# SSM operands put in order by block copies on chip, SSM products in column halves, and the cached keys' gain moved to the sampled queries

## The chip, the cores and the metric

The kernel runs on one core of a Trainium2 chip. A core has a matrix engine (TensorE, PE in the profile; its weight loads are listed as PEld), three engines for elementwise work (VectorE or DVE, ScalarE or ACT, GpSimd or POOL) and a queue engine that issues DMAs (SyncE, SP). ACT issues DMAs too. Each engine takes its own instructions in order and waits for the others by semaphores. The metric is the device time of one execution in microseconds; the median of several runs is compared.

## What is computed

One step of one decoder layer for 256 prompt tokens and 8 x 4 sampled tokens, d_model 2048, all in float32:

```python
x = x + 0.5 * swiglu(rms_norm(x))                 # first feed-forward, d_ff 5632
u, q, k, v = split(rms_norm(x) @ w_in)            # 1024 | 1024 | 256 | 256
y_ssm  = s5_mixer(u)     # 64 groups: 16 channels, 64 complex states; scan over positions
y_attn = window_attention(rms_norm(q, q_norm), rms_norm(k, k_norm), v)   # 16 heads, window 128
x = x + concat(rms_norm(y_ssm), rms_norm(y_attn)) @ w_out
x = x + 0.5 * swiglu(rms_norm(x))                 # second feed-forward
# s5_mixer:
h[t] = lam_bar * h[t-1] + B_bar u[t]
y = gelu(Re(C h) + D u);  y = y * sigmoid(y @ w_glu)
```

The sampled tokens see 128 cached keys of their sequence (already normed) and the 4 new ones. The kernel leaves the gain `q_norm` and the factor 1/8 out of the queries and applies both, as the column `qg`, to the other side of the score product.

## The kernel before

All 288 tokens (the sampled first in each group) stand as the columns of 128-row tiles. Every big product is an f32 product made of three passes over fp32r halves: for each weight piece of 128x1024, ScalarE casts the high half `wh` (L122), VectorE subtracts to get the low half `wl` (L123), and TensorE makes 24 products of 128x288 (L288 to L290).

**Slots.** The class `Weights` sets the order of the work. `W.next()` (one slot) issues the cast and subtraction of the piece two slots ahead (`split_ahead`), the loads of pieces five ahead, and then every function that was put in this slot with `W.at(slot, f)` in the order in which they were put; then the caller issues the slot's 24 products. `W.spread(slot, gen)` runs a generator one step a slot; with `last=True` its first step goes to the end of its slot. So side work stands in the queues of all engines between the big products, and what it waits for holds up what stands behind it on the same engine.

**The mixer** (`mix`, slots counted from `base`) projects in this order, two slots each: key pair 0, eight tiles of u, key pair 1, two tiles of v, eight tiles of q. Then 32 slots of `w_out`. R, the norm of x, is ready some slots in; until then evictions are held back (`Hold`).

**The SSM, tile j of 8.** The eviction (L756, VectorE) leaves u with channels on the partitions, for 4 quarters of 32 channels, and columns by position in a chunk of four. The products need it with 32 partitions for each position and the quarters side by side. Before, this order is made through DRAM: `ssm_u_store` (L759, issued on ACT's queue) and four loads of 32 partitions (L765, on SP's queue). In `ssm_state` (L790) eight matmuls of 128x128 by 128x72 give the chunk inputs; VectorE rotates them (L796 to L804), scans (L807, L808), rotates back (L817 to L821), with two products on POOL (L815, L816) and small copies on ACT and POOL. `ssm_out` (L830 to L832) makes twelve such matmuls, and ACT takes the gelu (L834). The result goes back to channel order through DRAM again: four stores (L840, ACT's queue), one load (L844, SP's queue) and, behind it on SP, the load of the gate weights `gl` (L846). `ssm_glu` multiplies by `gl` (L851), and `y_split` (L735 to L745) casts, squares and adds up. `state_done` and `ssm_done` free memory for the attention. With s = base + 2j + 5 the steps stand at s (store of u, first table load), s+2 (load of u, decay, rotation table), s+4 (state, four steps), s+6, s+9 (out), s+10, s+11 (store and load of y) and s+13 (gate).

**Attention, step i of 8** (a pair of heads). `q_square` (ACT), `scores`: sums of squares of the queries as two matmuls with the squares as the weights and two columns of `bones` (L1003), an inverse root in 12 small POOL instructions (`row_rsqrt`, L956 to L959), products with the keys (L1013), scaling (L1019), distance bias (L1023), softmax (L969 to L984, its last multiplication on POOL), then `probs_t` (transposes, L1032) and `pv` (L1045). The keys `kG` have been multiplied by `qg` on POOL (L909). For each key pair p, `sample` does the same for the sampled tokens with cached keys `ck`, which `cache_gain` multiplies by `qg` on POOL (L1060), and cached values (L1116).

## Time and profile before

| | |
|---|---|
| median of 3 runs | 1881.68 us (1880.63 to 1883.83) |
| the profiled execution | 1881.9 us, span 1880.1 us |
| PE busy | 1863.0 us (99%) |
| DVE, ACT, POOL busy | 1211.9, 850.6, 300.8 us |
| the 14400 big products (L288 to L290) | busy 4127.5 us by the sum of rows, each overlapping the next |
| SSM products, L790 and L830 to L832 | 320 instructions |
| granted TensorE clock | 1.00 |

The profile is one execution. A row of its groups names the line, the engine, the operation, what it writes and reads, its shape and its count, then busy time and mean length. The shape of a TensorE instruction has in front the part of the 128x128 array that it uses: `128*64` is all 128 rows and 64 columns. Lengths on TensorE are those of pipelined instructions: the next one starts before the last ends, so costs are read from starts. The matmuls of f32 stand in the trace as two instructions each. In the timeline, a row has its start, its length, and in brackets the idle time before it with what ended it.

### The profile page before, as it was taken

How to read it: one execution, taken by the hardware profiler on the slowest of the kernel's cores; microseconds unless marked ns; L12 is line 12 of the kernel's file. 1: busy time of each engine (PE TensorE's matmuls, PEld its weight loads, DVE VectorE, ACT ScalarE, POOL GpSimd, SP SyncE). 2: the span in 40 equal slices, each digit the busy share in tenths (PEclk: the TensorE clock that was granted, in tenths of full speed). 3: DMA queues.
4: the chain of work that ended last, by engine and by line, in shares of the span. 5: the costliest groups of instructions: out<-in, count | busy, mean ns of one | idle time of the engine just before them, and what ended most of it. 6: DMA issues, size and time to landing. Idle time of an engine off the chain costs nothing.

```text
span 1880.1 us, 37660 instructions
## 1 busy us (share of the span) xinstructions
PE 1863.0 (99%) x15264; PEld 1848.9 (98%) x15264; DVE 1211.9 (64%) x1877; ACT 850.6 (45%) x1337; POOL 300.8 (16%) x450
## 2 busy tenths in 40 slices
PE   9999999999999999999999999999999999999999
PEld 8999999999999999999988999999999999999999
DVE  6677667666667755687888885555555555555555
ACT  6443444444444444643476554433444334434433
POOL 3201011000100100211468650000000000000000
PEclk9999999999999999999999999999999999999999
DMA  7555656656665665778744456556655565556555
GB/s 265 198 181 165 217 179 213 196 170 218 213 200 171 213 213 156 238 246 290 239 137 133 158 176 183 180 165 183 191 180 171 170 197 180 167 167 205 180 162 170
DMA packets 123054, 359.04 MB, mean 191 GB/s; under 512 B 22496, under 2 KB 30688, under 8 KB 121696
## 3 DMA queue, kind: packets, MB, share of 16 engines
q1 hardware_dynamic: 114672, 340.48, 57.7%
q10 hardware_dynamic: 8208, 16.16, 2.5%
q8 instruction: 119, 1.95, 0.4%
q14 instruction: 55, 0.45, 0.1%
HBM read 338.40 MB, written 20.22 MB: 191 GB/s over the span
## 4 chain that ended last, share of the span: by engine, by line
PE 93%; DVE 2%; DMA 2%; POOL 2%; ACT 1%; issue 1%; SPq 0%; ACTq 0%; POOLq 0%; DVEq 0%
PE main L290 30%; PE main L288 30%; PE main L289 30%; DVE wl L123 1%; PE main L790 0%; DMA U<-ud 0%; PE main L832 0%; PE main L831 0%; PE main L621 0%; PE main L627 0%; PE main L830 0%; ACT wh L122 0%; POOL x L1153 0%; DMA out_kT<-s 0%; DVE sm_m L969 0%
## 5 line engine op out<-in xcount | busy, mean ns | idle before, releaser
L123 DVE TENSOR_TENSOR wl<-raw,wh 128x1024 fp32r<-128x1024 f32 (+2 forms) x677 | 751.7, 1111 | 453.9 <-ACT wh L122 451.6
L288 PE MATMUL main<-xh,wh 128*128 128x288 f32 x3136 | 902.5, 288 | 1.7 <-ACT xh L214 1.2
L290 PE MATMUL main<-xh,wl 128*128 128x288 f32 x3136 | 897.8, 286 | 0.7 <-DVE wl L123 0.6
L289 PE MATMUL main<-xl,wh 128*128 128x288 f32 x3136 | 897.3, 286 | 0.9 <-DVE xl L215 0.9
L122 ACT CAST wh<-raw 128x1024 fp32r<-128x1024 f32 (+2 forms) x677 | 636.9, 942 | 505.2 <-PE main L289 352.6
L288 PEld LDWEIGHTS main<-xh,wh 128*128 128x128 f32 x3136 | 592.8, 189 | 3.5 <-ACT xh L214 1.7
L289 PEld LDWEIGHTS main<-xl,wh 128*128 128x128 f32 x3136 | 592.8, 189 | 1.9 <-DVE xl L215 1.5
L290 PEld LDWEIGHTS main<-xh,wl 128*128 128x128 f32 x3136 | 592.7, 189 | 1.7 <-DVE wl L123 0.8
L288 PE MATMUL main<-hh,wh 128*128 128x288 f32 x1664 | 477.9, 287 | 1.2 <-DVE t L1152 0.7
L289 PE MATMUL main<-hl,wh 128*128 128x288 f32 x1664 | 476.0, 286 | 0.6 <-DVE hl L741 0.6
L290 PE MATMUL main<-hh,wl 128*128 128x288 f32 x1664 | 476.0, 286 | 0.0
L288 PEld LDWEIGHTS main<-hh,wh 128*128 128x128 f32 x1664 | 314.5, 189 | 1.8 <-DVE t L1152 0.9
L289 PEld LDWEIGHTS main<-hl,wh 128*128 128x128 f32 x1664 | 314.5, 189 | 1.0 <-DVE hl L741 0.8
L290 PEld LDWEIGHTS main<-hh,wl 128*128 128x128 f32 x1664 | 314.5, 189 | 0.2 <-DVE wl L123 0.2
L362 POOL TENSOR_TENSOR s<-s,R 128x288 f32<-128x288 f32 x88 | 70.7, 803 | 1139.2 <-ACT s L361 1139.2
L371 ACT CAST hh<-h 128x288 fp32r<-128x288 f32 x88 | 38.0, 432 | 222.9 <-DVE h L370 222.9
L361 ACT ACTIVATE s<-t 128x288 f32<-128x288 f32 x88 | 39.0, 443 | 219.9 <-DVE t L360 219.9
L392 DVE SCALAR_TENSOR_TENSOR x<-main,x 128x288 f32<-128x288 f32 x128 | 58.4, 456 | 39.9 <-PE main L290 39.5
L370 DVE TENSOR_TENSOR h<-main,s 128x288 f32<-128x288 f32 x88 | 40.1, 456 | 55.9 <-PE main L290 55.6
L360 DVE TENSOR_TENSOR t<-main,R 128x288 f32<-128x288 f32 x88 | 40.1, 456 | 45.1 <-PE main L290 44.7
L372 DVE TENSOR_TENSOR hl<-h,hh 128x288 fp32r<-128x288 f32 x88 | 40.3, 458 | 43.8 <-ACT hh L371 43.8
L224 POOL TENSOR_TENSOR acc<-acc,sq 128x288 f32<-128x288 f32 x45 | 45.3, 1006 | 46.0 <-ACT sq L220 45.1
(268 smaller groups left out, 913.9 us busy)
## 6 DMA issues: line engine op xcount, KB each, us to landing
raw<-in_w_gu SPq DMA_DIRECT2D x349, 512.0 KB, 3.9
raw<-in_w_dn SPq DMA_DIRECT2D x128, 384.0 KB, 3.1
raw<-in_w_dn SPq DMA_DIRECT2D x128, 320.0 KB, 3.2
raw<-in_w_in SPq DMA_DIRECT2D x40, 512.0 KB, 4.5
raw<-in_w_out SPq DMA_DIRECT2D x32, 512.0 KB, 3.4
mats<-stage ACTq DMA_DIRECT2D x8, 1536.0 KB, 6.8
mb<-mats SPq DMA_DIRECT2D x8, 768.0 KB, 6.2
ma<-mats SPq DMA_DIRECT2D x8, 512.0 KB, 4.2
```

Of the source, the lines that this page charges most:

```text
L122: self.nc.scalar.copy(wh[:, :n], t[:, :n])
L123: self.nc.vector.tensor_tensor(wl[:, :n], t[:, :n], wh[:, :n].bitcast(F32), op=ALU.subtract)
L224: eng.tensor_tensor(acc, acc, sq, op=ALU.add)
L288: pe.matmul(ps, wh[:, s], woven(rh[k]), start=first and a == 0, stop=False)
L289: pe.matmul(ps, wh[:, s], woven(rl[k]), start=False, stop=False)
L290: pe.matmul(ps, wl[:, s], woven(rh[k]), start=False, stop=last and a == n - 1)
L360: dve.tensor_tensor(t1, pg[:, :N], R, op=ALU.mult)
L361: act.activation(s1, t1, AF.Silu)
L362: pool_e.tensor_tensor(s2, s1, R, op=ALU.mult)
L370: dve.tensor_tensor(halved(h), evens(pu[:, :N]), evens(s2), op=ALU.mult)
L372: dve.tensor_tensor(hl, h, hh.bitcast(F32), op=ALU.subtract)
L392: dve.scalar_tensor_tensor(x[d], ps[:, :N], 0.5, x[d], op0=ALU.mult, op1=ALU.add)
```

## The change

Four parts:

1. *Order by copies.* The DRAM scratch goes. `turn` copies a tile in 16 blocks of 32 partitions by 72 columns, block (b, a) to block (a, b): u on ACT (`ssm_turn_u`), y on POOL (`ssm_turn_y`). The load of `gl` stands alone in `ssm_glu_load`.
2. *Halves.* The SSM products and the sums of squares of the queries use 64 columns of the array at a time (`HALVES`), so each matmul becomes two, on column halves 0 to 63 and 64 to 127.
3. *Order of steps.* With s = base + 2j + 4 (one slot earlier) the steps stand at s (first table load; turn of u, but at s+1 for j below 2), s+1 (rotation table), s+2 (state, no longer last in its slot), s+4, s+7 (out), s+8 (turn of y), s+9 (`gl`), s+11 (gate). The end of the SSM and its norm come three slots earlier. In attention, the first step of `scores` now stands before `probs_t` in its slot and after `pv`, where it stood behind both. `d0` has one buffer instead of two, `yg` two instead of one.
4. *Gain.* `cache_gain` goes. The sampled queries are multiplied by `qg` on ACT after their squares were taken, and `kG` has the gain on its prompt columns alone; its sampled columns are a plain copy.

```diff
@@ -36,6 +36,7 @@
 PSUM = bass.MemoryType.PSUM
 DRAM = bass.MemoryType.DRAM
 SLOPES = [float(np.float32(2.0 ** (-8.0 * (h + 1) / NH))) for h in range(NH)]
+HALVES = (slice(0, 64), slice(64, 128))
 MAGIC = 1.5 * 2.0 ** 23
 TWO_PI = 6.283185005187988
 
@@ -716,8 +717,6 @@
     vT = mp.tile([P, 2, N], F32, name="vT")
     V = mp.tile([P, 2, 256], F32, name="V")
     Vs = mp.tile([T * NB, 256], F32, name="Vs")
-    ud = [dr.tile([P, N], F32, name="ud%d" % j) for j in range(8)]
-    yd = [dr.tile([P, N], F32, name="yd%d" % j) for j in range(8)]
 
     def consts():
         get(cst, io["mix_cst"])
@@ -755,14 +754,15 @@
         UE[j] = tp.tile([P, N], F32, name="t1")
         tt(UE[j], ps[:, :N], R, op=ALU.mult)
 
-    def ssm_u_store(j):
-        put(ud[j], UE.pop(j))
-
-    def ssm_u_load(j):
+    def turn(copy, out, src):
+
+        for a in range(4):
+            for b in range(4):
+                copy(out[32 * a:32 * a + 32, b], src[32 * b:32 * b + 32, a])
+
+    def ssm_turn_u(j):
         U[j] = sm.tile([P, 4, W1], F32, name="U", bufs=4)
-        src = ud[j].rearrange("(q c) (j t) -> j c q t", q=4, j=T)
-        for jr in range(T):
-            get(U[j][32 * jr:32 * jr + 32], src[jr])
+        turn(act.copy, U[j], UE.pop(j).rearrange("p (j t) -> p j t", j=T))
 
     def ssm_load_a(j):
         MA[j] = sa.tile([P, 2, 4, P], F32, name="ma", bufs=2)
@@ -773,7 +773,7 @@
         get(ROT[j].rearrange("p q s k -> p (q s k)"), e["mats"][j][:, 2560:])
 
     def ssm_decay(j):
-        D0[j] = sa.tile(c4, F32, name="d0", bufs=2)
+        D0[j] = sa.tile(c4, F32, name="d0", bufs=1)
         act.copy(D0[j], e["e4"][:, 4 * j:4 * j + 4, None].to_broadcast(c4))
         pool_e.memset(D0[j][:, :, 0:1], 0.0)
 
@@ -787,7 +787,8 @@
         for i in range(2):
             ps = aux()
             for q in range(4):
-                pe.matmul(ps[:, q * W1:(q + 1) * W1], ma[:, i, q], u[:, q], start=True, stop=True)
+                for hh in HALVES:
+                    pe.matmul(ps[hh, q * W1:(q + 1) * W1], ma[:, i, q, hh], u[:, q], start=True, stop=True)
             b.append(ps[:, :N].rearrange("p (q t) -> p q t", q=4))
         br, bi = b[0][:, :, NB:], b[1][:, :, NB:]
         co, si = rot[:, :, 0, :], rot[:, :, 1, :]
@@ -826,22 +827,17 @@
         mb, u, cs = MB.pop(j), U.pop(j), CS.pop(j)
         ps = aux()
         for q in range(4):
-            o = ps[:, q * W1:(q + 1) * W1]
-            pe.matmul(o, mb[:, 0, q], u[:, q], start=True, stop=False)
-            pe.matmul(o, mb[:, 1, q], cs[:, 0, q, :W1], start=False, stop=False)
-            pe.matmul(o, mb[:, 2, q], cs[:, 1, q, :W1], start=False, stop=True)
-        YG[j] = sm.tile([P, 4, W1], F32, name="yg", bufs=1)
+            for a, rhs in enumerate((u[:, q], cs[:, 0, q, :W1], cs[:, 1, q, :W1])):
+                for hh in HALVES:
+                    pe.matmul(ps[hh, q * W1:(q + 1) * W1], mb[:, a, q, hh], rhs, start=a == 0, stop=a == 2)
+        YG[j] = sm.tile([P, 4, W1], F32, name="yg", bufs=2)
         act.activation(YG[j].rearrange("p q t -> p (q t)"), ps[:, :N], AF.Gelu_apprx_tanh)
 
-    def ssm_y_store(j):
-        yg = YG.pop(j)
-        dst = yd[j].rearrange("(q c) (j t) -> j c q t", q=4, j=T)
-        for jr in range(T):
-            put(dst[jr], yg[32 * jr:32 * jr + 32])
-
-    def ssm_y_load(j):
+    def ssm_turn_y(j):
         YN[j] = sm.tile([P, N], F32, name="yn", bufs=2)
-        get(YN[j], yd[j])
+        turn(pool_e.tensor_copy, YN[j].rearrange("p (j t) -> p j t", j=T), YG.pop(j))
+
+    def ssm_glu_load(j):
         GL[j] = sm.tile([P, P], F32, name="gl", bufs=2)
         get(GL[j], io["w_glu"][j])
 
@@ -871,21 +867,20 @@
     hold = e["Hold"](W.i + 2)
     consts()
     for j in range(8):
-        s = base + 2 * j + 5
-        W.at(s, ssm_u_store, j)
+        s = base + 2 * j + 4
         W.at(s, ssm_load_a, j)
-        W.at(s + 2, ssm_u_load, j)
+        W.at(s + 1, ssm_load_r, j)
+        W.at(s + (1 if j < 2 else 0), ssm_turn_u, j)
+        W.spread(s + 2, ssm_state(j))
         W.at(s + 2, ssm_decay, j)
-        W.at(s + 2, ssm_load_r, j)
-        W.spread(s + 4, ssm_state(j), True)
-        W.at(s + 6, ssm_load_b, j)
-        W.at(s + 9, ssm_out, j)
-        W.at(s + 10, ssm_y_store, j)
-        W.at(s + 11, ssm_y_load, j)
-        W.spread(s + 13, ssm_glu(j))
-    W.at(s + 8, state_done)
-    W.at(s + 17, ssm_done)
-    W.spread(s + 18, e["norm"](e["ones"], acc, R_ssm, 1.0 / 1024, 4 * EPS))
+        W.at(s + 4, ssm_load_b, j)
+        W.at(s + 7, ssm_out, j)
+        W.at(s + 8, ssm_turn_y, j)
+        W.at(s + 9, ssm_glu_load, j)
+        W.spread(s + 11, ssm_glu(j))
+    W.at(s + 7, state_done)
+    W.at(s + 15, ssm_done)
+    W.spread(s + 16, e["norm"](e["ones"], acc, R_ssm, 1.0 / 1024, 4 * EPS))
 
     def tok(ap, blk):
 
@@ -906,7 +901,9 @@
         yield
         kT = tp.tile([P, N], F32, name="s1")
         stt(kT, kr, gains[:, 65:66], rk, op0=ALU.mult, op1=ALU.mult)
-        pool_e.tensor_scalar(kG[:, p], kT, qg, None, op0=ALU.mult)
+        chunks = [v.rearrange("p (j t) -> p j t", j=T) for v in (kG[:, p], kT)]
+        pool_e.tensor_scalar(*(v[:, :, NB:] for v in chunks), qg, None, op0=ALU.mult)
+        pool_e.tensor_copy(*(v[:, :, :NB] for v in chunks))
         yield
         put(io["kT"][p], kT)
 
@@ -992,16 +989,19 @@
         p, g = divmod(i, 4)
         if g == 3:
             s2 = mp.tile([P, P], F32, name="qssq")
-            act.activation(s2, QS[p][0].rearrange("p b g j -> p (b g j)"), AF.Square)
-            QS[p] = (QS[p][0], s2)
+            qs = QS[p][0].rearrange("p b g j -> p (b g j)")
+            act.activation(s2, qs, AF.Square)
+            act.activation(qs, qs, AF.Copy, scale=qg)
+            QS[p] = (qs, s2)
 
     def scores(i):
         p, g = divmod(i, 4)
         qb, sq = QN.pop(i)
         pq = aux()
         for blk in range(2):
-            pe.matmul(pq[:, 2 * blk:2 * blk + 2], sq[:, 128 * blk:128 * blk + 128],
-                      bones[:, 0:128:64], start=True, stop=True)
+            for hh in HALVES:
+                pe.matmul(pq[hh, 2 * blk:2 * blk + 2], sq[:, 128 * blk:128 * blk + 128][:, hh],
+                          bones[:, 0:128:64], start=True, stop=True)
         v = mp.tile([P, 4], F32, name="rq_v", bufs=4)
         ts(v, pq[:, :4], 1.0 / 64, EPS, op0=ALU.mult, op1=ALU.add)
         rq = row_rsqrt(v, 4)
@@ -1056,12 +1056,8 @@
         CV[p] = late["y"].tile([P, NB, P], F32, name="cv")
         get(CV[p], io["cache_vr"][p])
 
-    def cache_gain(p):
-        pool_e.tensor_scalar(CK[p], CK[p], qg, None, op0=ALU.mult)
-
     def sample(p):
         qs, sq = QS.pop(p)
-        qs = qs.rearrange("p b g j -> p (b g j)")
         ps = aux()
         v = mp.tile([P, 2], F32, name="rq_v", bufs=4)
         pe.matmul(ps[:, :2], sq, bones[:, 0:128:64], start=True, stop=True)
@@ -1125,17 +1121,18 @@
                 next(y, None)
             yield
 
-    for i in range(8):
-        s = base + 2 * (12 + i) + 2
+    S = [base + 2 * (12 + i) + 2 for i in range(8)]
+    for i, s in enumerate(S):
         W.at(s, q_square, i)
-        W.spread(s + 1, scores(i), True)
+        W.at(s + 11, pv, i)
+    for i, s in enumerate(S):
+        W.spread(s + 1, scores(i))
+    for i, s in enumerate(S):
         W.at(s + 9, probs_t, i)
-        W.at(s + 11, pv, i)
     for p in range(2):
         s = base + 2 * (12 + 4 * p + 3) + 2
         W.at(s - 4, cache_k_load, p)
         W.at(s + 4, cache_v_load, p)
-        W.at(s, cache_gain, p)
         W.spread(s + 2, sample(p))
     for i in range(8):
         p, g = divmod(i, 4)
```

## The prediction

> **What bounds the kernel now.** I read the page's first part, then the table of stages (busy time per stretch), the waits of TensorE, the timeline around every place where its stream of big products is broken, and the groups of instructions of the other engines.
>
> ```profile
> PE 1863.0 (99%) x15264; PEld 1848.9 (98%) x15264; DVE 1211.9 (64%) x1877; ACT 850.6 (45%) x1337; POOL 300.8 (16%) x450
> ...
> 590.00:806.00 216.00, 216.00 (x1761) 215.79 (x1760) 136.61 (x210) 107.58 (x173) 26.76 (x33) 1.00 0.66 208
> 820.00:960.00 140.00, 134.65 (x1132) 131.16 (x1130) 111.40 (x226) 61.07 (x129) 46.09 (x103) 1.00 0.76 247
> ...
> PE main L790 <- DMA U<-ud: 3.0, 2, 2.0
> PE main L1032 <- POOL lg L984: 1.5, 2, 1.0
> PE main L851 <- DMA gl<-in_w_glu: 1.4, 1, 1.4
> PE main L1003 <- DVE rq_v L1068: 1.4, 1, 1.4
> ```
>
> In the stage rows the columns are the stretch and its length, then busy time of PE, PEld, DVE, ACT, POOL, the granted clock (1.00 throughout), DMA share, GB/s. TensorE never rests in the feed-forward stretch. In the mixer's SSM stretch, 820 to 960, it lacks 5.35 us, and the four waits quoted lie there and in the attention behind it, where the change lies too. So the time changes by what TensorE's own instructions cost, plus what it waits for in the mixer; a saving on another engine counts only through a wait. VectorE is 80% busy (111.4 of 140) in the SSM stretch: close behind.
>
> **TensorE's products.** A busy row overlaps its neighbour, so I cost by start to start, from the last big product before a group to the first one after.
>
> ```profile
> 855.38 0.29 PE L290 MATMUL main<-xh,wl 128*128 128x288 f32 x1
> 855.51 1.90 PE L790 MATMUL main<-U,ma 128*128 128x72 f32 x16
> 857.21 0.37 PE L288 MATMUL main<-xh,wh 128*128 128x288 f32 x1
> 857.42 0.29 PE L289 MATMUL main<-xl,wh 128*128 128x288 f32 x1
> ...
> 860.11 0.29 PE L290 MATMUL main<-xh,wl 128*128 128x288 f32 x1
> 860.23 0.34 PE L830 MATMUL main<-U,mb 128*128 128x72 f32 x2
> ...
> 862.83 0.37 PE L288 MATMUL main<-xh,wh 128*128 128x288 f32 x1
> ...
> 974.35 0.29 PE L290 MATMUL main<-xh,wl 128*128 128x288 f32 x1
> 974.57 0.94 PE L1013 MATMUL main<-kG,qn 64*128 64x128 f32 x12
> 975.43 0.39 PE L288 MATMUL main<-xh,wh 128*128 128x288 f32 x1
> 975.66 0.29 PE L289 MATMUL main<-xl,wh 128*128 128x288 f32 x1
> ...
> 978.57 0.88 PE L1045 MATMUL main<-pt,V 128*64 128x128 f32 x12
> L1045 PE MATMUL main<-pt,V 128*64 128x128 f32 x96 | 7.0, 281 | 0.0
> ...
> 1035.23 1.11 PE L1116 MATMUL main<-pc,cv 128*64 128x16 f32 x32
> L1116 PE MATMUL main<-pc,cv 128*64 128x16 f32 x64 | 2.2, 210 | 0.0
> ```
>
> Big products follow each other by 0.122 (857.42 to 860.11 is 22 of them), so one slot of 24 takes 2.94. The state group of a tile (L790, 16 instructions, two for each f32 matmul) takes 857.21 - 855.38 = 1.83, less 0.12 for the big product that it follows, plus 0.08 for the late second one: 1.79, or 0.112 each. The output group (L830 to L832, 24) takes 862.83 - 860.11, so corrected, 2.68: 0.112 each again. Eight tiles: 35.8 us.
>
> In halves the instructions double, and two with different column halves can be in the array together. L1045 has that form with 128 moving columns: 12 instructions last 0.88, of which the last one's own length (mean 281 ns) is no step; that leaves 0.60 over 5.5 steps, 0.11 a pair. L1116, with 16 columns: 1.11 less 0.21 over 15.5 steps, 0.058 a pair. With 72 columns, proportional to the first (72/128 of 0.110) it is 0.062, just over the second; on a straight line between both it is 0.084. I take 0.062, because the longer row looks stream-bound, and keep 0.058 to 0.084. Changing the array's shape costs too: L1013 alone takes 975.43 - 974.35 = 1.08, less 0.12, plus 0.11 late start of the second big product, 1.07, for 6 pairs of 0.11 = 0.66. So 0.41 a group; I take 0.38, since pairs of columns show a slightly quicker entry.
>
> State group: 16 x 0.062 + 0.38 = 1.37 instead of 1.79. Output group: 24 x 0.062 + 0.38 = 1.87 instead of 2.68. Eight tiles: 8 x (0.42 + 0.81) = 9.8; I book -9.5. At 0.084 a pair it is -2.3, at 0.058 about -11. [...]
>
> The query sums of squares (L1003, 4 instructions of two columns) become 4 pairs, 0.23 with 0.38 where the shape changes. They now stand ahead of the probability transposes and next to the L1045 pairs, so later heads change shape once anyway. Five heads lose about 0.2, three gain 0.2: +0.4.
>
> **The waits that go.** The round trips through DRAM delayed TensorE at three places.
>
> ```profile
> 843.83 0.29 PE L290 MATMUL main<-xh,wl 128*128 128x288 f32 x1
> 845.09 1.98 PE L790 MATMUL main<-U,ma 128*128 128x72 f32 x16 [0.97 <-DMA U<-ud]
> ...
> 865.73 0.29 PE L290 MATMUL main<-xh,wl 128*128 128x288 f32 x1
> 868.02 1.98 PE L790 MATMUL main<-U,ma 128*128 128x72 f32 x16 [2.01 <-DMA U<-ud]
> ...
> 872.70 0.29 PE L290 MATMUL main<-xh,wl 128*128 128x288 f32 x1
> 874.38 0.72 PE L851 MATMUL main<-yn,gl 128*128 128x288 f32 x2 [1.40 <-DMA gl<-in_w_glu]
> ```
>
> Start to start, less 0.12: 1.14 + 2.17 + 1.56 = 4.9 us. The load of `gl` was late because it stood on SP behind the load of `yn`, which waits for a store; that load is gone. Booked -4.9 (0 at worst, if something else is as late). From tile 2 on the block copies have two whole slots, so I expect nothing in its place there.
>
> In attention, TensorE waits on POOL's probabilities and on a sample's norm, 1.5 + 1.4. Ahead of both on POOL stands the scaling of the cached keys, which goes:
>
> ```profile
> L1060 POOL TENSOR_SCALAR ck<-ck,qg x2: 2838/2848/2858, 949.5 to 993.5; 128x1024 f32<-128x1024 f32 x2
> ```
>
> Two times 2.85 us leave POOL. Its replacement is one small ScalarE pass over 128x128 a key pair, several slots ahead of its reader: nothing. I book -2.0 of the 2.9 (0 to -4: such a gap hides a late restart). Splitting the key scaling into a scaled part and a copy adds one short POOL instruction a pair, long before the first score.
>
> **The block copies of u, on ScalarE.**
>
> ```profile
> 816.14 1.99 ACT L122 CAST wh<-raw 128x1024 fp32r<-128x1024 f32 x2
> 816.65 0.50 PE L288 MATMUL main<-xh,wh 128*128 128x288 f32 x1
> 818.36 0.45 DVE L756 TENSOR_TENSOR t<-main,R 128x288 f32<-128x288 f32 x1
> ...
> L642 ACT COPY stage<-km 32x64 f32<-32x64 f32 x16 | 3.9, 243 | 0.2
> ...
> 882.99 0.22 ACT L812 COPY cs<-h 128x32 f32<-128x32 f32 x1
> 883.11 0.22 ACT L813 COPY cs<-h 128x32 f32<-128x32 f32 x1
> ```
>
> A 32x64 copy lasts 0.243, but two neighbours (L812, L813) start 0.12 apart. Sixteen copies of 32x72 take 2.7 us at 0.17 apart, 4.0 if nothing overlaps; I take 2.7. Five DMA issues a tile leave the ScalarE queue, so its load hardly rises, and the weight casts behind a turn have two slots of lead.
>
> For tiles 0 and 1 there is one slot, not two. The first turn stands in the slot whose big products start at 816.65; the next slot starts at about 819.8, and with it now the state products of tile 0 (formerly three slots later). The evicted u is ready at 818.81 (L756), the casts ahead on ScalarE end at 818.13. The turn ends at 818.9 + 2.7 = 821.6: TensorE waits 1.8 (3.1 at 4.0). Tile 1: its slot starts at 821.6 + 1.37 + 2.94 = 825.9; a cast of 1.0 must go first because its buffer comes free only then; the turn ends at 829.6, the products are due at 828.9: 0.7 to 2.0. Together +2.6 (1 to 5.1). Queued behind those products are all big ones; nothing else covers it.
>
> **The block copies of y, on POOL, and the earlier start.** The SSM work of VectorE is not reduced but squeezed: TensorE would spend about 11 us less in a stretch where VectorE is busy 111.4 of 140, and the first tiles now meet the first key norm.
>
> ```profile
> L608 POOL COPY rep<-bb x32: 231/238/1239, 179.1 to 619.8; 64x64 f32<-64x64 f32 x32
> ...
> L608 POOL COPY rep<-bb 64x64 f32<-64x64 f32 x32 | 11.1, 376 | 0.7
> ...
> 883.15 0.75 POOL L815 TENSOR_TENSOR ra<-ra,rot 128x256 f32<-128x256 f32 x1
> 883.23 0.95 DVE L817 TENSOR_TENSOR cs<-ra,rot 128x256 f32<-128x256 f32 x1
> ...
> L820 DVE TENSOR_TENSOR cs<-cs,ra 128x256 f32<-128x256 f32 x8 | 3.3, 416 | 0.0
> ```
>
> A copy of this kind costs 0.24 by the median, 0.38 by the mean. L817 beside a POOL instruction lasts 0.95, the same shape alone 0.42: the two engines hold each other up. With 128 copies added, half of them meeting VectorE and costing it 0.12, VectorE has 119 us of work in some 129: peaks will be late. All 128 at 0.24, 80% of them met, would make it 136 in 129. I book +3 (0 to +8).
>
> **Sum**, against the profiled execution's own 1881.9 (its span is 1880.1, and 1.8 lie around it): -9.5 + 0.4 - 4.9 - 2.0 + 2.6 + 3.0 = -10.4, so 1871.5. The median of the three runs, 1881.68, is 0.2 lower; I predict 1871.3. Its own range is 1864 to 1877.
>
> **Rivals.** *POOL becomes the bound of the SSM stretch (slower).* A tile then takes TensorE 2 x 2.94 + 1.37 + 1.87 + about 0.5 = 9.6. POOL was busy 46.09 in the SSM stretch, at most 5.8 a tile; some of that belongs to scores and to the key scaling, so I take two thirds, 3.9. Sixteen copies fit while each takes under 0.36 (5.7 us). Each that waits out a VectorE instruction takes longer (the maximum of L608 is 1.24). At 0.5 a copy POOL is 2.3 late a tile, 16 us in seven, and the gated product L851 waits: 1871.3 - 3 + 16 = 1884. It turns slower from 0.48 on. For it: the mean of 0.38 with VectorE less loaded than here. Against: VectorE's instructions that read the product's buffer, and its idle fifth, leave POOL room. [...] Chance 0.12.
>
> *The halves do not pair* (the change does not do what it says): one after the other, a pair takes 0.124, and 320 pairs add 0.062 each: 1891; at the straight line's 0.084, 1878. Against: the L1045 and L1116 rows. Chance 0.08.
>
> *The turn of u is late for every tile*, because the eviction that it waits for stands behind a late VectorE: about 1 us for six more tiles, 1877. Chance 0.09.
>
> *Halves at twice the speed*, no price for the change of shape: 8.4 more gained, 1863. Chance 0.07. The forecast keeps 0.64.
>
> **How the numbers follow.** About 0.2%, 3.8 us, is what a measurement of this kernel can tell from no change. Faster by more (under 1877.9): nearly all of the forecast, the twice-speed case, half of the late turn: 0.75. Within: 0.12, from the straight line and mild POOL lateness. Slower: 0.13, from a severe one and unpaired halves. The range 1863 to 1881 leaves out most of these last.
>
> **What would show it.** Right: L790 and L831 rows in halves, starts 0.062 a pair; no wait on DMA `U` or `gl`; a first state group that waits for ScalarE by 1 to 3 us; no L1060. Wrong: pairs over 0.09 apart; TensorE waiting at L851 for POOL's `yn`; POOL copies of 0.4 us and more; waits on `wl` between 820 and 960.

## The result and the profile after

The changed kernel takes 1897.38 us (median of 4 runs, 1894.35 to 1898.71) against 1881.68 for the kernel before on the same chip (median of three): 1.0079 times as long, 95% interval 1.0059 to 1.0099. Three slow runs are left out here and below, one of 3425.55 us of the kernel before, one of 2131.63 of `e9` and one of 3244.78 of `e15`, which was the profiled one (granted clock 0.556), so that `e15` has no trace to read. The change is about 15 us slower, where 10 us less was forecast. The profiled execution takes 1896.9, its span is 1895.1. The lines of the changed kernel are shifted: the big products are L289 to L291, the casts L123 and L124, the copies of both turns L761, the state products L791, the output products L832, the gate product L847.

The first part of the page after, the SSM stretch in the columns shown before, and the first rows of TensorE's waits from 800 to 1150 us:

```profile
PE 1864.6 (98%) x15616; PEld 1844.3 (97%) x15616; DVE 1205.2 (64%) x1877; ACT 881.7 (47%) x1467; POOL 340.9 (18%) x578
```

```profile
820.00:960.00 140.00, 121.78 (x1330) 112.33 (x1329) 100.46 (x205) 79.66 (x223) 81.31 (x211) 0.93 0.56 201
```

```profile
PE main L791 <- DMA ma<-mats: 6.0, 2, 3.8
PE main L847 <- POOL yn L761: 4.5, 2, 3.1
PE main L791 <- ACT U L761: 3.7, 2, 2.3
PE main L832 <- DVE cs L821: 2.6, 3, 1.7
PE main L1032 <- POOL lg L981: 2.4, 2, 1.8
```

In the SSM stretch TensorE lacks 18.2 us where it lacked 5.35; POOL rose from 46 to 81 of 140; and the granted clock is 0.93 where it was 1.00. All waits of TensorE between 800 and 1150 add up to 24.4 us, against 9.9 before. The waits for `U<-ud` and `gl` are gone; in their place stand the table `ma`, POOL's `yn`, ScalarE's `U` and VectorE's `cs`.

The products themselves did what was forecast. An undisturbed state group and output group on TensorE:

```profile
839.37 0.29 PE L291 MATMUL main<-xh,wl 128*128 128x288 f32 x1
839.59 1.22 PE L791 MATMUL main<-U,ma 128*64 128x72 f32 x32
840.74 0.39 PE L289 MATMUL main<-xh,wh 128*128 128x288 f32 x1
...
843.66 0.29 PE L291 MATMUL main<-xh,wl 128*128 128x288 f32 x1
843.88 0.35 PE L832 MATMUL main<-U,mb 128*64 128x72 f32 x4
...
844.68 0.29 PE L832 MATMUL main<-U,mb 128*64 128x72 f32 x4
...
845.05 0.29 PE L832 MATMUL main<-U,mb 128*64 128x72 f32 x4
...
845.53 0.39 PE L289 MATMUL main<-xh,wh 128*128 128x288 f32 x1
```

From start to start the state group takes 840.74 - 839.37 = 1.37, with the same corrections as in the prediction 1.35 (before 1.79); the output group 1.87, corrected 1.85 (before 2.68). Twelve instructions, six pairs, take 845.05 - 844.68 = 0.37: 0.062 a pair. Over eight tiles that is 8 x (0.44 + 0.83) = 10.2 us less.

Where does POOL lose the time? Its timeline over two tiles, start and length, and in brackets the idle time ahead with what ended it:

```profile
887.41 0.52 POOL L824 COPY fin<-cs 128x4 f32<-128x4 f32 x2 [0.35 <-DVE cs L821]
891.89 5.98 POOL L761 COPY yn<-yg 32x72 f32<-32x72 f32 x16 [3.97 <-DVE s L852]
...
897.98 0.11 POOL L812 MEMSET cs<- 128x8 f32 x1
898.16 1.12 POOL L816 TENSOR_TENSOR ra<-ra,rot 128x256 f32<-128x256 f32 x1
899.25 1.10 POOL L817 TENSOR_TENSOR ra<-ra,rot 128x256 f32<-128x256 f32 x1
...
906.06 2.30 POOL L761 COPY yn<-yg 32x72 f32<-32x72 f32 x4 [4.61 <-DVE s L852]
```

And the group of all copies of y, with the idle time ahead of them:

```profile
L761 POOL COPY yn<-yg 32x72 f32<-32x72 f32 x128 | 44.0, 344 | 20.9 <-DVE s L852 16.0
```

Ahead of its sixteen copies POOL stands still for 3.97 and 4.61 us, 16.0 us in all, and what it waits for is VectorE's L852, the instruction of the gate that reads `yn`. `yn` has two buffers, so the copies of tile j+2 may not begin before VectorE has read `yn` of tile j. Before, the load of `yn` stood one slot behind that reading. Now, with the copies of tile j+2 at base + 2(j+2) + 4 + 8 and the gate's second step at base + 2j + 4 + 12, both stand in the same slot, and what waits is not a DMA queue but an engine with work behind it. VectorE in the same stretch:

```profile
891.32 0.45 DVE L852 SCALAR_TENSOR_TENSOR s<-s,yn 128x288 f32<-128x288 f32 x1
...
898.08 0.69 DVE L808 TENSOR_TENSOR_SCAN ra<-d,ra 128x256 f32<-128x256 f32 x1 [2.25 <-POOL cs L812]
...
904.15 0.42 DVE L797 TENSOR_TENSOR ra<-main,rot 128x256 f32<-128x256 f32 x1
...
905.48 0.45 DVE L852 SCALAR_TENSOR_TENSOR s<-s,yn 128x288 f32<-128x288 f32 x1
```

That closes a ring: L852 frees the buffer, six microseconds of copies follow, behind them POOL clears an edge of `cs` (L812), VectorE's scans (L808) wait 2.25 us for POOL, and behind the scans come the next tile's rotation and the next L852, 14.2 us after the last one. That is the longest of the seven steps; on average L852 comes every 11.2 us (877.9 to 956.2). TensorE needs 9.6 us a tile, by the prediction's own sum. VectorE's waits for that memset from 820 to 960, and a wait on SP, which is caught too:

```profile
DVE ra L808 <- POOL cs L812: 6.7, 3, 3.1
```

```profile
SPq L773 <- POOL ra L817: 25.9, 4, 8.0
```

The rotation table's load (L773) waits 8 us at the worst for a buffer that POOL's L817 frees, and the load of `ma`, for which TensorE waits 3.84 us at 872.97, stands behind it on SP.

Some of the waits cost a second time. In these rows the columns are again the stretch, its length, the busy time of PE, PEld, DVE, ACT and POOL, the granted clock, DMA share and GB/s. Stretches around two such waits:

```profile
868.00:873.00 5.00, 1.16 (x12) 0.97 (x11) 2.60 (x6) 3.81 (x10) 4.54 (x13) 1.00 0.58 220
873.10:876.50 3.40, 3.40 (x38) 3.25 (x38) 3.40 (x7) 1.28 (x5) 0.51 (x2) 0.50 0.65 215
876.60:880.00 3.40, 3.40 (x41) 3.02 (x42) 2.45 (x8) 3.19 (x15) 1.34 (x4) 1.00 0.95 347
911.00:914.00 3.00, 1.03 (x6) 0.49 (x6) 1.75 (x3) 1.05 (x2) 2.74 (x8) 1.00 0.42 165
914.10:920.80 6.70, 5.51 (x54) 5.16 (x55) 6.67 (x13) 1.19 (x3) 4.04 (x8) 0.50 0.28 81
```

TensorE rests nearly four of the five microseconds from 868 to 873; then its clock is granted at one half for 3.4 us, later for 6.8. Four such stretches add up to 20.5 us, each behind one or two waits; the profiled execution of the kernel before has none. At half speed they cost at most 10.2 us. With that upper bound the books close within half a microsecond: 14.5 us more waiting, 10.2 for the clock, 10.2 less for the products, 14.5 in all, against 15.0 by the two profiled executions.

### The profile page after: what moved, and what is told of

It reads as the page before. It is cut to its first block, busy times and chain, and to the rows that moved or that the text cites. A ratio compares the mean times of both kernels' runs of the same rounds, so it can differ in the third digit from the quotient of the medians.

```text
span 1895.1 us, 38494 instructions
## 1 busy us (share of the span) xinstructions
PE 1864.6 (98%) x15616; PEld 1844.3 (97%) x15616; DVE 1205.2 (64%) x1877; ACT 881.7 (47%) x1467; POOL 340.9 (18%) x578
## 4 chain that ended last, share of the span: by engine, by line
PE 47%; POOL 3%; DVE 2%; DMA 1%; issue 1%; ACT 1%; SPq 0%; POOLq 0%
PE main L289 15%; PE main L290 15%; PE main L291 15%; POOL yn L761 1%; DMA ma<-mats 1%; DVE wl L124 1%; POOL lg L981 0%; POOL x L1150 0%; ACT wh L123 0%; ACT lg L974 0%; POOL rq_o L956 0%; DVE sm_m L966 0%; PE main L791 0%; DVE lg L1023 0%; POOL acc L744 0%
## 5 line engine op out<-in xcount | busy, mean ns | idle before, releaser
L124 DVE TENSOR_TENSOR wl<-raw,wh 128x1024 fp32r<-128x1024 f32 (+2 forms) x677 | 752.1, 1111 | 451.4 <-ACT wh L123 447.9
L289 PE MATMUL main<-xh,wh 128*128 128x288 f32 x3136 | 906.4, 289 | 1.6 <-ACT lg L1019 1.2
L291 PE MATMUL main<-xh,wl 128*128 128x288 f32 x3136 | 900.6, 287 | 0.5 <-DVE wl L124 0.4
L123 ACT CAST wh<-raw 128x1024 fp32r<-128x1024 f32 (+2 forms) x677 | 636.9, 942 | 488.2 <-PE main L290 329.7
L289 PEld LDWEIGHTS main<-xh,wh 128*128 128x128 f32 x3136 | 595.7, 190 | 5.0 <-ACT lg L1019 1.4
L291 PEld LDWEIGHTS main<-xh,wl 128*128 128x128 f32 x3136 | 595.5, 190 | 1.5 <-DVE wl L124 0.6
L289 PE MATMUL main<-hh,wh 128*128 128x288 f32 x1664 | 477.9, 287 | 0.0
L291 PE MATMUL main<-hh,wl 128*128 128x288 f32 x1664 | 476.0, 286 | 0.0
L289 PEld LDWEIGHTS main<-hh,wh 128*128 128x128 f32 x1664 | 314.5, 189 | 0.5
L291 PEld LDWEIGHTS main<-hh,wl 128*128 128x128 f32 x1664 | 314.5, 189 | 0.2 <-DVE wl L124 0.2
```

Of the source, the lines that this page charges most:

```text
L123: self.nc.scalar.copy(wh[:, :n], t[:, :n])
L124: self.nc.vector.tensor_tensor(wl[:, :n], t[:, :n], wh[:, :n].bitcast(F32), op=ALU.subtract)
L289: pe.matmul(ps, wh[:, s], woven(rh[k]), start=first and a == 0, stop=False)
L291: pe.matmul(ps, wl[:, s], woven(rh[k]), start=False, stop=last and a == n - 1)
```

## The experiments

Every ratio is to the kernel before, run on the same chip (medians 1881.97 to 1882.97), with its 95% interval. In the expectations, theory A is that the POOL copies of y pace the tiles, and theory C that TensorE waits because `ma` is loaded behind the rotation table on SP. The theory of the buffer is formed further down, where the runs on ScalarE call for it.

**y through DRAM again (changed kernel otherwise).**

```diff
-        W.at(s + 8, ssm_turn_y, j)
+        W.at(s + 8, ssm_y_store, j)      # four stores, ACT's queue
+        # load of yn in ssm_glu_load, at s + 9, SP's queue
```

> The changed kernel with only the turn of y taken back to DRAM (four stores on ScalarE's queue, one load on SP, the gate weights loaded ahead of it); u is still turned by copies, products in halves, new schedule. Theory A (the sixteen POOL copies a tile make POOL the bound of the SSM stretch; everything late there comes from them): 1882.8 before, less 10.2 for the halves, less about 5 for the waits on DRAM, less 2 in attention, plus about 4 for the first two turns of u: 1870, between 1866 and 1875, and no half clock. Theory B (the earlier start squeezes VectorE and ScalarE, whoever turns y): still above 1885.

1878.89, ratio 0.9983 (0.9974 to 0.9993). The POOL copies cost 18.5 us; no wait for `yn` or `gl` is left. Of the changes, only some 3 us of gain remain: that is far from theory B's 1885, but also above the 1866 to 1875 of theory A, and the trace still has 3.4 us at half clock twice.

**`ma` two slots earlier.**

```diff
-        W.at(s, ssm_load_a, j)
+        W.at(s - 2, ssm_load_a, j)
```

> The changed kernel with the load of the state table ma two slots earlier, so that it no longer stands on SP behind the load of the rotation table, which waits for POOL. Theory A (POOL itself is the bound): the waits on ma (6.0 us) go, but TensorE then waits for POOL's yn and for cs instead; 1890 to 1897. Theory C (POOL is late but harmless, and the loss is SP standing still): the waits on ma and the half clock that follows them go, 1880 to 1886.

1897.14, ratio 1.0082 (1.0067 to 1.0097). TensorE's waits, first rows:

```profile
PE main L832 <- DVE cs L821: 6.8, 6, 1.7
PE main L847 <- POOL yn L761: 5.3, 3, 3.1
```

The wait for `ma` is gone and its time stands at `cs` and `yn` instead. C fell: the late load was where the ring showed, not what drove it.

**Each gain alone.** The halves alone, put into the kernel before:

```diff
-                pe.matmul(ps[:, q * W1:(q + 1) * W1], ma[:, i, q], u[:, q], start=True, stop=True)
+                for hh in HALVES:
+                    pe.matmul(ps[hh, q * W1:(q + 1) * W1], ma[:, i, q, hh], u[:, q], start=True, stop=True)
...
```

> The kernel before with nothing but the SSM products in halves. Each state group 0.44 and each output group 0.83 shorter as the changed kernel's trace shows: 10.2 us, 1872.5 if nothing else is late. If the round trips through DRAM are what paces the tiles, TensorE waits longer for U and gl and half of it is lost: 1877.

1879.47, ratio 0.9990 (0.9980 to 0.9999). TensorE's waits:

```profile
PE main L792 <- DMA U<-ud: 5.5, 4, 2.5
PE main L852 <- DMA gl<-in_w_glu: 4.5, 3, 2.2
```

10.2 us fewer of products, by the group costs of the changed kernel, but only 2.5 us less time, less than either expectation: the waits for the round trips through DRAM, 3.0 and 1.4 before, are 5.5 and 4.5 now. These two account for 5.6 of the 7.7 us that are lost on the way.

The gain on the sampled queries alone, put into the kernel before:

```diff
-        W.at(s, cache_gain, p)
...
+            act.activation(qs, qs, AF.Copy, scale=qg)
```

> The kernel before with nothing but the gain moved to the sampled queries (no cache_gain on POOL). If the 2.85 us instruction is what makes POOL late in attention: 2 us less, 1880.5. If those waits come from VectorE: no difference, 1882.8.

1879.97, ratio 0.9989 (0.9980 to 0.9999): 2.0 us, with the waits on POOL's probabilities and on L1003 gone. The profiled execution was the slowest of the ten (1882.26, with 6.8 us at half clock behind a wait of 2.8 for `U`), so its trace shows which waits go, and not the gain.

**The rest of the order of steps.** First the old order of the attention's steps on top of the kernel with y through DRAM, then also all SSM steps but the turn one slot later, so that the first two turns have a slot more:

```diff
-            W.spread(s + 1, scores(i))
+            W.spread(s + 1, scores(i), True)
```

> The kernel e1_y_dram with the attention steps registered as before (the first step of scores again last in its slot, behind the probability transposes). e1 still waits 2.5 + 1.7 us for POOL's probabilities and runs 3.4 us at half clock there; the kernel with the gain alone waits 0.7. If the new order is the cause: 3 to 6 us less than e1's 1878.9, so 1873 to 1876. If the earlier start of the SSM is the cause: no difference.

```diff
-        s = base + 2 * j + 4
+        s = base + 2 * j + 5
-        W.at(s + (1 if j < 2 else 0), ssm_turn_u, j)
+        W.at(s - (1 if j else 0), ssm_turn_u, j)
```

> The kernel e5_old_scores with all SSM steps but the turn of u one slot later, so that every tile has two slots between its turn and its state products. If the first two turns cost what the trace of e1 shows (4.1 + 3.2 us of wait, and 1.7 for the half clock behind the first, less what the old schedule spent there) it is 5 to 7 us below e5: 1867 to 1870. If VectorE is what is late at the start: no difference.

1878.46 (0.9977, 0.9967 to 0.9986) and 1877.82 (0.9977, 0.9967 to 0.9986). Neither makes a difference that can be told from the run without it, so the 3 to 6 and the 5 to 7 us that I had thought possible did not come. In the second the two waits for `U` ahead of the first state products are gone, but one of 3.3 us came ahead of the output products.

**One POOL copy instead of sixteen.** The same bytes; the order of y is left as it is, so this kernel leaves out the turn of y.

```diff
-        turn(pool_e.tensor_copy, YN[j].rearrange("p (j t) -> p j t", j=T), YG.pop(j))
+        pool_e.tensor_copy(YN[j], YG.pop(j).rearrange("p q t -> p (q t)"))
```

> The changed kernel with the sixteen POOL copies of y replaced by a single copy of 128x288, which leaves the order of y as it is: the same bytes, 15 instructions fewer a tile, no DMA. Theory A (the number of short POOL instructions, about 0.28 each in a row with VectorE waiting behind them, is the bound): as e1, 1877 to 1881, and no wait on ma, yn or cs. If the bytes or the port are the bound, or the missing DRAM trip is not what helped e1: above 1890.

1877.19, ratio 0.9970 (0.9958 to 0.9981). From POOL's timeline:

```profile
886.72 0.82 POOL L838 COPY yn<-yg 128x288 f32<-128x288 f32 x1 [3.07 <-DVE s L852]
...
887.52 0.11 POOL L812 MEMSET cs<- 128x8 f32 x1
```

I read this as proof that the number of POOL instructions alone is the cause. But the row shows more: the wait for the buffer is still there (3.07 here, 20.4 us in six waits, more than in the changed kernel), and it does little harm when the memset comes 0.8 us behind it instead of 6. VectorE no longer waits for the memset in this trace. So the wait alone costs little; what counts is the block of copies behind it.

**A pause of TensorE, measured by itself.** In the second feed-forward of the kernel before: six pauses, each two small products with 1 to 11 ScalarE copies between them.

```diff
+            pe.matmul(ps[:, :N], ident, x[0], start=True, stop=True)
+            act.copy(chain, ps[:, :N])
+            for _ in range(n):
+                act.copy(chain, chain)
...
+            pe.matmul(pt[:, :N], ident, chain, start=True, stop=True)
```

> The kernel before with six pauses of TensorE in the second feed-forward, 24 slots apart: a product, a chain of 1, 3, 5, 7, 9 and 11 ScalarE copies of 0.45 us, and a product that needs the last one. It measures what a wait costs beyond itself. Waits of about 0.9, 1.8, 2.7, 3.6, 4.5, 5.4 and 0.5 of products each: 1882 + 22 = 1904 if a wait costs itself. If the clock falls to half behind the longer ones, for 3.4 or 6.8 us each as in the changed kernel's trace: 1.7 or 3.4 more for three or four of them, 1909 to 1917.

1921.26, ratio 1.0207 (1.0191 to 1.0222): 39 us more, while the waits for the copies add up to 22. Even the expectation with the clock, 1909 to 1917, was too low. The fourth pause in stretches:

```profile
1355.00:1361.00 6.00, 6.00 (x52) 6.00 (x51) 2.91 (x3) 2.42 (x3) 0.80 (x1) 1.00 0.58 177
1361.00:1365.00 4.00, 0.75 (x5) 0.29 (x3) 2.14 (x3) 3.01 (x7) 0.00 (x0) 1.00 0.55 178
1365.00:1372.00 7.00, 5.64 (x21) 5.35 (x22) 0.00 (x0) 1.65 (x4) 0.00 (x0) 0.52 0.23 75
```

Around the end of 4.62 us without work the clock falls to one half for 6.8 us, although nothing of the mixer is near. Pauses of 2.99 and 3.91 us from start to start left the clock alone, one of 3.61 cost 3.4 us of half clock, those of 6.1 to 7.0 cost 6.8 each.

**The old order of steps with the gains.** Once with u by ScalarE copies and y through DRAM, once with both through DRAM; both with halves, the gain moved and `gl` loaded ahead.

```diff
+        W.at(s + 9, ssm_glu_load, j)
-        W.at(s, ssm_u_store, j)
+        W.at(s, ssm_turn_u, j)           # only in the first of the two
...
```

> The kernel before in its old schedule, with those parts of the change that the runs so far speak for: SSM products in halves, u turned by copies on ScalarE (four slots ahead of its product, U in five buffers), the gain on the sampled queries; y stays on the trip through DRAM, with the gate weights loaded ahead of it; sums of squares and scores as before. Theory A with the waits added up: 1882 less 10.2 for the halves, less 3.3 for U, less 1 to 1.6 for gl, less 2 in attention: 1865 to 1868. If the trip of y paces the tiles (as gl did in e3_halves, 4.5 us): 1870 to 1873.

> As e9_old_schedule, but u too goes through DRAM as before: the difference of the two is what the copies of u are worth. In e3_halves TensorE waited 5.5 us for U. If that is their worth: 4 to 6 us above e9, 1871 to 1874. If the copies only shift the wait to ScalarE: the same.

1877.38 (0.9973, 0.9962 to 0.9984) and 1877.30 (0.9971, 0.9960 to 0.9982). The copies of u on ScalarE are worth nothing that can be measured, and I missed the 1865 to 1868 that I had expected of the first: halves and the gain bring 5.6 us of their 12.

**Full-width products, and `fin` on VectorE, in the changed kernel.**

```diff
-                for hh in HALVES:
-                    pe.matmul(ps[hh, q * W1:(q + 1) * W1], ma[:, i, q, hh], u[:, q], start=True, stop=True)
+                pe.matmul(ps[:, q * W1:(q + 1) * W1], ma[:, i, q], u[:, q], start=True, stop=True)
...
```

> The changed kernel with the SSM products in full 128 columns again (halves undone). If TensorE were the bound there, this costs 10.2 us: 1907. Theory A (POOL and what waits for it set the pace): the products fill time in which TensorE waits anyway, and its idle stretches get shorter, so the clock falls less often: 1892 to 1899.

```diff
-            pool_e.tensor_copy(fin[:, i, q], cs[:, i, :, W1])
+            dve.tensor_copy(fin[:, i, q], cs[:, i, :, W1])
```

> The changed kernel with the two small copies of the final state moved from POOL to VectorE. On POOL they wait for VectorE's last step of a tile, and the sixteen copies of y stand behind them, so POOL and VectorE take turns: copies, two products, VectorE, final state, copies, 10.8 us a round by the trace. If this ring is the bound: without it POOL needs about 9 a tile, under TensorE's 9.7, and the kernel falls to 1880 to 1888. If the sheer number of POOL instructions is the bound: 1893 to 1897.

1900.07 (1.0092, 1.0079 to 1.0105) and 1896.85 (1.0073, 1.0060 to 1.0087). Ten microseconds more of TensorE work cost 2.7, a microsecond more than theory A gave: TensorE is not what paces the tiles there. The second was my ring through `fin`, and it fell. What POOL waited for in that kernel told where the ring really goes:

```profile
POOL yn L761 <- DVE s L852: 23.9, 5, 8.0
```

With the `fin` copies off POOL, the wait for the buffer of `yn` grew from 16.0 to 23.9.

**Only y by POOL copies, on the old order with u through DRAM.**

```diff
-        W.at(s + 10, ssm_y_store, j)
-        W.at(s + 11, ssm_y_load, j)
+        W.at(s + 10, ssm_turn_y, j)
```

> The order of steps of before, with halves, the gain on the sampled queries and the load of gl ahead; u goes through DRAM as before, and only y is turned by 16 POOL copies, in the slot of its former stores. Theory (the number of POOL instructions in the SSM stretch paces the tiles): 6 to 20 us more than the same kernel with y through DRAM (1877.3), so 1883 to 1897, with TensorE waiting on POOL for yn or for rotation tables, or for ma behind them. Rival (the copies cost so much only because all steps stand a slot earlier and u is turned by copies too): 1876 to 1880.

1884.87 (1.0011, 1.0000 to 1.0021): 7.6 us more than the same kernel with y through DRAM, in the lower half of what theory A gave. Here too the copies share a slot with L852 (17.3 us of waits, five times), and because this kernel has one `yg`, ScalarE waits for POOL:

```profile
ACT yg L835 <- POOL yn L842: 21.6, 4, 9.3
```

The tiles keep their pace until slot 26; the lateness then comes out at once, as a 6.1 us wait of TensorE for a ScalarE result of the attention, with 10.2 us at half clock behind it (granted clock 0.83 from 910 to 940).

**The copies of y on ScalarE, and shared by both engines (changed kernel).**

```diff
-        turn(pool_e.tensor_copy, YN[j].rearrange("p (j t) -> p j t", j=T), YG.pop(j))
+        turn(act.copy, YN[j].rearrange("p (j t) -> p j t", j=T), YG.pop(j))
```

> The changed kernel with the 16 copies of y on ScalarE instead of POOL: 34 us of copies move from POOL (81 busy of 140 in the SSM stretch) to ScalarE (80 of 140). Theory (POOL's own queue is the bound): about the time of the kernels that leave the POOL copies out, 1877 to 1882, perhaps a little more for weight casts that now stand behind copies. Rival (sixteen copies in a row are too long for any engine, because TensorE's products wait for the last one): 1888 to 1900, with waits on ACT for yn, U or wh.

```diff
+                (act.copy if b % 2 else pool_e.tensor_copy)(yv[32 * a:32 * a + 32, b], yg[32 * b:32 * b + 32, a])
```

> The changed kernel with eight of the sixteen copies of y on ScalarE and eight on POOL. If POOL is a bound with a threshold, as the tile's 10.8 us against TensorE's 9.7 suggest, 2.2 us a tile less on POOL takes all of the loss away: 1877 to 1882. If each POOL copy has a price of its own (it holds up VectorE, or VectorE it), half of the loss of 19 is left: 1886 to 1890.

1915.38 (1.0172, 1.0150 to 1.0193) and 1896.90 (1.0074, 1.0049 to 1.0100). Both went against theory A: with no copy on POOL the loss doubled, with half of them there it stayed. ScalarE's first wait in the first:

```profile
ACT yn L761 <- DVE s L852: 25.7, 6, 6.1
```

It is the same buffer, now stopping the engine that also casts the weights and turns u. That made the new theory: not POOL's load, but a wait for `yn` in the queue of an engine that others need.

**The wait removed, all 128 copies left on POOL.** By a third buffer of `yn` (paid for with one of `yg`), and by one slot:

```diff
-        YG[j] = sm.tile([P, 4, W1], F32, name="yg", bufs=2)
+        YG[j] = sm.tile([P, 4, W1], F32, name="yg", bufs=1)
-        YN[j] = sm.tile([P, N], F32, name="yn", bufs=2)
+        YN[j] = sm.tile([P, N], F32, name="yn", bufs=3)
```

> The changed kernel with three buffers of yn instead of two, and one of yg instead of two to make room; 16 POOL copies a tile as they are. New theory (the ring through the buffer: POOL stops up to 4.6 us ahead of the copies of tile j+2, until VectorE has read yn of tile j in L852, and the 6 us of copies, the memset of cs and the two rotation products then stand behind; VectorE's scans, and behind them L852 of the next tile, wait for those): the wait of POOL for VectorE's s goes, 1879 to 1886 with some lateness where ScalarE's gelu now waits for the one yg. Rival (the mere number of POOL instructions): 1894 to 1900 as the changed kernel.

```diff
-        W.at(s + 8, ssm_turn_y, j)
+        W.at(s + 9, ssm_turn_y, j)
```

> The changed kernel with the copies of y one slot later, at s+9 instead of s+8, so that in the queues they stand a slot behind the VectorE instruction L852 that frees their buffer; the gate stays at s+11, with two slots for the copies. Same buffers, same 128 POOL copies. New theory (POOL stands waiting for the buffer with the rotation products behind it): most of the loss goes, 1877 to 1884. Rival (number of POOL instructions; a slot less before the gate makes yn later): 1895 to 1905.

1886.43 (1.0026, 1.0017 to 1.0036) and 1883.56 (1.0005, 0.9996 to 1.0015): 11 and 13.8 us less than the changed kernel, where the rival had them at 1894 and more. In the first no wait for `yn` is left, but the one `yg` gives ScalarE a new wait for POOL (19.4 us). POOL's wait for `yn`, and its timeline, in the second:

```profile
POOL yn L761 <- DVE s L852: 0.5, 1, 0.5
```

```profile
898.21 0.74 POOL L817 TENSOR_TENSOR ra<-ra,rot 128x256 f32<-128x256 f32 x1
...
899.95 8.35 POOL L761 COPY yn<-yg 32x72 f32<-32x72 f32 x16
908.36 0.69 POOL L824 COPY fin<-cs 128x4 f32<-128x4 f32 x2
```

The wait for the buffer is down from 16.0 to 0.5, and VectorE's waits for POOL's memset are gone in both traces. What is left is POOL's own load: no gap between the instructions around the copies, 0.52 a copy in this tile, and TensorE waits 7.2 us for `yn`.

**That, with every second copy on ScalarE.** The two edits of `e15` and `e17` together.

> The kernel of e17_turn_later (copies of y at s+9, no wait for their buffer) with every second copy on ScalarE: same number of copies, half of POOL's. In e17_turn_later POOL is busy 26.9 of 30 us from 880 to 910, its 16 copies last 6.6 to 8.4 us a tile, and TensorE waits 7.2 us for yn. If what is left of the loss is POOL's own load, these waits go: 1875 to 1880, unlike e15_y_both, where the same division changed nothing. If the copies cost the same on any engine: 1883 to 1890.

1876.92, ratio 0.9965 (0.9951 to 0.9978). TensorE's waits:

```profile
PE main L791 <- ACT U L761: 3.7, 2, 2.3
...
PE main L850 <- POOL yn L841: 1.8, 1, 1.8
```

The division that did nothing while the buffer wait stood takes 6.6 us away once it is gone. This kernel computes all of the reference and has the lowest time of those that do, about 0.35% below the kernel before, though the two with DRAM (1877.3 and 1877.4) can't be told from it.

## Why the prediction was wrong

**The step that failed** is the booking of the POOL copies of y, "+3 (0 to +8)". It was sized by what the copies would cost VectorE; no sentence of the prediction asks what the copies themselves wait for. "From tile 2 on the block copies have two whole slots, so I expect nothing in its place there" looks only ahead, at who waits for the copies, and by its "from tile 2 on" it speaks of u. The change put a wait for the buffer of `yn` on POOL's queue. Before, the load of `yn` stood one slot behind the reading that frees the buffer, and its waits on SP were for other transfers, the store `yd<-yg` above all, not for that reading. The diff gives `yg` a second buffer and leaves `yn` at two, and the slots of copy and reading could be counted from it. By the runs the copies cost 18.5 us (y through DRAM) to 20 us (one copy): 13.8 of them go with the wait (one slot later), and 6.6 more with half of POOL's load.

So of the 26.1 us between forecast and result, 15.5 are this term (18.5 instead of 3). The other 10.6 are savings that did not reach the time: without the copies of y the sum gives 1868.3, and `e1` took 1878.9.

**The rival that came nearest** is the one of 0.12, POOL as the bound. It had the place and the sign, and one of the prediction's signs of being wrong came with it, TensorE waiting for POOL's `yn` (4.5 us). But it did not have the mechanism: its price of 16 us came from POOL's own load, with a threshold of 0.36 a copy, and in the changed kernel a copy lasts 0.344, below it. That 16 lies near the measured 18.5 is luck. As a load it is real, but small: it is the 6.6 us that are left when the wait is gone, with 5.6 to 8.4 us for sixteen copies where 5.7 would have fitted.

**The halves** were right: 10.2 against 9.5, 0.062 a pair, 0.062 measured. Twice the speed, the last of the rivals, did not come: the two groups are 1.33 and 1.45 times as fast (1.79 against 1.35 us, 2.68 against 1.85), and no run shows a factor of 2. (At 0.084 a pair the prediction's own working gives 2.8, not 2.3; nothing else changes by that.) What failed is the way from there to the time. Alone they give 2.5 us of the 10.2, because the waits for the round trips, 4.4 us before, are 10 when the tile is shorter. I had put the saving and the waits down as terms that add up; here the waits took most of the saving back.

**The DRAM waits** of 4.9 went as predicted, but taking out those for u brought nothing that the two runs on the old order show: with u by copies 1877.4, through DRAM 1877.3.

**The gain**, booked at -2.0, gave 2.0 alone. **The first two turns of u**, booked at +2.6 with 0.17 a copy, took 4.20 us for sixteen on ScalarE, 0.26 apart: just above the 4.0 that I gave for no overlap. TensorE waited 2.33 by the row below, and 3.7 in all for both tiles; counted from start to start, 2.84 and 1.9.

```profile
822.78 1.66 PE L791 MATMUL main<-U,ma 128*64 128x72 f32 x32 [2.33 <-ACT U L761]
...
824.37 0.39 PE L289 MATMUL main<-xh,wh 128*128 128x288 f32 x1
```

```profile
819.35 4.20 ACT L761 COPY U<-t 32x72 f32<-32x72 f32 x16 [0.71 <-DVE t L755]
```

**The clock** was no term at all. That the best kernel stays 5.6 us above my 1871.3 fits it: its trace has 13.7 us at half clock in the mixer, up to 6.8 us of loss. That is a sum, not an experiment: no run took the clock away and left the waits. Open too is why the two kernels on the old order bring only 5.6 of about 12 us; their traces show new single waits of 3.1 to 3.4 us (for `yn`, for a query's square, for VectorE) and 10.2 and 6.8 us at half clock, and none of these was tried by itself.

## What to carry to other kernels

When a step moves from a DMA queue to an engine, write down what it waits for as well as who waits for it: the buffer that it writes, who reads that last, and in which slot. Here y was written three slots ahead of its gate, where it had been loaded two ahead, and two buffers did not carry that; the wait then stood in front of six microseconds of work that others needed. When a run takes away a suspected load and the time stays, look at what the loaded engine was waiting for just ahead of it. And a saving on the bound engine is worth only what its next wait lets through, so try it alone before adding it to a sum.

## What the runs showed of the hardware

A wait of TensorE can cost it again afterwards. In these traces the granted clock then stands at one half for 3.4 or 6.8 us, in `e13` also for 10.2, and in `e14` it is 0.81 over the 30 us from 880 to 910; in the run with the pauses the big products are then 0.24 apart instead of 0.123. A stretch of 3.4, 6.8 or 10.2 costs at most 1.7, 3.4 or 5.1 us. The length of the wait alone does not decide it. The first wait for the turned `U`, 2.3 us, stands in eleven traces: behind it the clock fell in seven (`e1`, `e11`, `e12`, `e14`, `e16`, `e17`, `e18`) and stayed in four (the changed kernel, `e2`, `e5`, `e8`); over the 30 us from 820 to 850 it is 0.94 in `e1`, `e14` and `e17`, and 1.00 in the changed kernel and `e8`. Stretches behind this wait in `e17`, where it ends at 822.0, and in the changed kernel, where it ends at 822.8:

```profile
823.20:826.50 3.30, 3.30 (x27) 3.15 (x23) 2.69 (x7) 0.94 (x2) 0.10 (x1) 0.50 0.53 174
```

```profile
823.00:830.00 7.00, 7.00 (x78) 6.72 (x75) 5.67 (x13) 4.25 (x12) 0.10 (x1) 1.00 0.73 262
```

In the changed kernel the four stretches last 3.413, 3.413, 6.827 and 6.827 us, and the later three begin 23.89, 40.96 and 64.85 us after the first, which is 7, 12 and 19 times 3.413. Among the pauses one of 3.91 us passed unpunished and one of 3.61 did not. What sets the lengths and the places was not shown.

In the changed kernel the small copies from one group of 32 partitions to another did not overlap: sixteen took 4.20 us on ScalarE (0.249 each) and 4.4 to 8.9 on POOL, where one lasts 0.238 by the median and up to 1.246. Nine of POOL's copies there last over 1.1 us. Each of them starts while VectorE's L124 runs, which reads `raw` and `wh` and writes `wl`, and ends 0.10 us behind it; in these nine rows POOL is the one that waits. Eight others overlap, of VectorE's instructions, L797 to L800 alone, which read `main` and `rot`; they last 0.233 to 0.236.
